# Differences of the values moved into the convolution stage, and queries and keys of two heads split together with their rows placed by DMA

## The chip, the cores and the metric

The kernel runs on one core of one Trainium2 chip. The metric is the time of one execution in microseconds of the device. Before the change three timed runs took 2573.38, 2568.3 and 2574.95 us, the median is 2573.38. One further execution was profiled.

## What is computed

The reference is one layer of a hybrid decoder trunk on x of 1024 tokens by 1024 channels, in float32. The change lies in its first sub-layer, parallel token mixing. One input projection of the normalised stream gives q, k and v of 16 attention heads of 64 dimensions, the inputs z, x, B, C and dt of a state-space mixer (SSD), and two gates, ga and gs. The x|B|C channels go through a causal convolution over 4 tokens and a silu. The attention is of the stick-breaking kind:

```
z = einsum('bhtd,bhsd->bhts', qf, kf)            # qf scaled by 64 ** -0.5
log_1mb = where(causal, log_sigmoid(-z), 0.0)
tail = cumsum(log_1mb, axis=3, reverse=True)
w = where(causal, exp(z + tail), 0.0)
out = einsum('bhts,bhsd->bhtd', w, v)
```

The outputs of attention and mixer are projected, gated and summed. Cross-attention into 256 memory tokens and a SwiGLU feed-forward follow.

The kernel computes the product of (1 - beta) from the right by a scan: with c[t, s] the product over j >= s of sigmoid(-z), the weight w[t, s] is c[t, s+1] - c[t, s]. So the sum over s of w[t, s] v[s] can be written with the differences v[s] - v[s+1], or rather of neighbouring rows of v, and c - 1. The "differences" below are these: rows r of v_d less rows r + 1, where v_d is v in DRAM with one row more.

## The kernel before the change

Every matmul is made in a reduced float32 format (F32R). An operand is split into a high half, its value rounded to F32R, and a low half, what is left of it, and a product takes three matmuls (high by high, low by high, high by low) or, where the two halves are stacked on the 128 rows that are contracted, two. The helpers are `hi_sb` (line 87), which writes a high half on POOL ("p"), DVE ("v") or ACT ("a"), and `lo_of` (line 98), which subtracts it from the value, on DVE or POOL.

The program is written with tile pools; the order of the instructions on each engine is set by a scheduler that follows the order of the code by its priorities, and a tile that is asked for from a full pool waits until the oldest one is released. All DMAs of the stages here are issued on SP's queue in order.

The work runs in stages, by the trace: norms, transposes and token-major projections (z, v) to 270 us; the convolution stage, 270 to 642 us; the attention, 624 to 1083 us, overlapping a little with its neighbours; SSD to 1480 us; output projections, cross-attention and feed-forward to the end at 2567 us.

**The convolution stage.** It makes 18 calls of `pair` (line 681). A pair computes 256 channels for all 1024 tokens with seven products in place of eight, each of 12 matmuls of 128x512 (`winograd_pair`, L226; matmuls L220 to L222), out of weights prepared by `winograd_weights` (L188): two loads of 512 KB (`wr`), four sums on POOL (`sf`, L196 to L199), then for each of seven operands a high half on ACT (L96) and a low half on DVE (L99) into `sw`. The products leave PSUM by three ACT copies (L230, L232, L234) and three DVE additions (L237, L239, L241) and one more ACT copy (L688) into two tiles of 128x1024, `y`, from the pool "b4" with six buffers. Twelve pairs are x|B|C channels, for which `conv` takes a further b4 buffer and makes three shifted multiply-adds on DVE (L667), the sigmoid on ACT (L668), and the product on DVE (L669); `tail` transposes the result in the next pair. Six pairs are gates: a sigmoid (L678) and a store to g_d (L679). The list `order` mixes them, one gate pair after every two of the others, with the last gate pair at the end.

**The attention.** It goes over 16 heads in eight pairs. A pair's q and k come from `qk_proj` (L782): `dense` (L758) makes 24 matmuls of 128x512 for each half of the tokens, so that a PSUM tile holds 64 rows of one head over 64 rows of the other. `ev_q` copies each head's rows to the upper half of its tile `qs` on ACT (L794) and writes the low half below it on DVE (L795). `ev_k` writes the high half into the upper rows of `kh` (L806) and the low half into those of `kl` (L807), and a DMA copies each to the lower 64 rows (L808, L809), so that two matmuls make a score: the stacked q with `kh` twice over, and with `kl` twice over.

A head is worked through in two m-steps, one per half of the tokens, so a pair has four. In each, `interleave` mixes three lists: `values` for this m-step, `scores` for the next one, and a quarter of the q and k projections of a later pair. `scores` has four blocks of two matmuls per 512 keys (L849, L850), a sigmoid on ACT (L851) and a scan on DVE over up to 1024 keys (L852, with the 0/1 tile `mask`). `values` transposes the result (L868), writes high and low halves `wth` on ACT (L871) and `wtl` on DVE (L872), and makes two matmuls with `v` (L880, L881), three steps behind the transposes; ACT and DVE bring the result out (L888, L889).

`differences` (L822) provides `v`. For each pair it loads two shifted tiles `va` and `vb` of 512 KB (L828), subtracts them on POOL (L829), and for each head writes the high half (L92) and the low half (L99) on POOL into a tile of two buffers.

## Time and profile before

| | |
|---|---|
| three timed runs | 2573.38, 2568.3, 2574.95 us |
| profiled execution | 2569.1 us, span 2567.4 us |
| mean granted clock of TensorE | 0.993 |
| busy: PE, DVE, ACT, POOL | 2485.3, 1817.7, 1149.7, 824.6 us |
| convolution window 280 to 640: PE, DVE, ACT, POOL | 356.33, 266.19, 193.84, 112.27 us |
| attention window 690 to 1000: PE, DVE, ACT, POOL | 299.81, 273.42, 195.80, 57.13 us |
| PE's wait for DVE in the attention window | 11.0 us |

A row of a group reads: line, engine, operation, output and inputs by the program's names, shape, count, then busy time and the mean of one in ns, then the idle time of the engine just before these instructions with what ended it. A row of the waits reads: who waited for whom, us in total, times, and the longest. A row of a timeline gives the start, the duration, and in brackets the idle time before with what ended it. "SPq" is the queue of SyncE, which issues the DMAs.

### The profile page before, as it was taken

Reading aid. Unit: us, or ns where it says so; the run is one execution under the profiler, and the core shown is the slowest. Engines: PE = TensorE matmul, PEld = TensorE weight load, DVE = VectorE, ACT = ScalarE, POOL = GpSimd, SP = SyncE. Lnnn points to the kernel's source line nnn. Section 1 sums busy time; section 2 is a strip of 40 time slices with the busy share of each in tenths; the row PEclk is TensorE's granted clock in tenths of the full one; section 3 lists DMA queues with packets and bytes.
Section 4 is the critical chain, followed back from the end, with each engine's and each line's share of the span. In section 5 each row is a group of like instructions: output and inputs, shape, how many; then the busy total and the mean of one; then the engine's idle time right before and its main releaser. Section 6 shows DMA issues by size and latency. Waiting matters only on the chain.

```text
span 2567.4 us, 32619 instructions
## 1 busy us (share of the span) xinstructions
PE 2485.3 (97%) x12026; PEld 2059.4 (80%) x12026; DVE 1817.7 (71%) x2143; ACT 1149.7 (45%) x2052; POOL 824.6 (32%) x666
## 2 busy tenths in 40 slices
PE   8999999999999999989999999999999999999998
PEld 6788788887788788777888788888787888887776
DVE  7685777767689898678788654415459666666997
ACT  6343455655466666556544302314233333334433
POOL 4331533221211121135655231100114333333675
PEclk9999999999999999989999999999999999999999
DMA  6441433333322222355332452321332232234322
GB/s 227 148 154 58 152 123 99 109 109 121 99 79 67 83 73 63 102 161 185 112 93 71 148 176 94 116 63 36 115 111 70 79 95 74 88 93 164 132 99 99
DMA packets 244331, 278.54 MB, mean 108 GB/s; under 512 B 15040, under 2 KB 171849, under 8 KB 243787
## 3 DMA queue, kind: packets, MB, share of 16 engines
q1 hardware_dynamic: 244170, 276.45, 34.0%
q8 instruction: 95, 1.56, 0.2%
q14 instruction: 66, 0.53, 0.1%
HBM read 197.87 MB, written 70.13 MB: 104 GB/s over the span
## 4 chain that ended last, share of the span: by engine, by line
PE 37%; DVE 7%; DMA 3%; issue 2%; POOL 1%; ACT 1%; SPq 0%; POOLq 0%; DVEq 0%; ACTq 0%
PE mm L222 5%; PE mm L220 5%; PE mm L221 5%; PE mm L102 4%; PE mm L104 3%; PE mm L103 3%; PE p L102 2%; PE p L103 2%; PE p L104 2%; DVE op L99 2%; PE pd L1090 1%; DMA gr<-gu_d 1%; DVE a L1755 1%; PE p L1468 1%; DMA wraw<-in_w_mix_out_dram 1%
## 5 line engine op out<-in xcount | busy, mean ns | idle before, releaser
L852 DVE TENSOR_TENSOR_SCAN n<-n,mask 128x128 f32<-128x128 f32 (+7 forms) x128 | 176.4, 1403 | 11.9 <-ACT n L851 9.2
L196 POOL TENSOR_TENSOR sf<-wr,wr 128x512 f32<-128x512 f32 x38 | 60.4, 1590 | 351.5 <-DMA wr<-in_w_gu_dram 129.3
L99 DVE TENSOR_TENSOR sw<-sf,sw 128x512 fp32r<-128x512 f32 x150 | 111.4, 754 | 58.9 <-ACT sw L96 58.4
L871 ACT ACTIVATE wth<-tr,mone 128x512 fp32r<-128x512 f32 x192 | 110.9, 580 | 73.3 <-PE tr L868 71.6
L96 ACT ACTIVATE sw<-sf 128x512 fp32r<-128x512 f32 x150 | 92.1, 626 | 106.8 <-PE mm L222 95.3
L872 DVE SCALAR_TENSOR_TENSOR wtl<-tr,wth 128x512 fp32r<-128x512 f32 x192 | 101.5, 546 | 40.0 <-ACT wth L871 38.5
L96 ACT ACTIVATE sw<-wr 128x512 fp32r<-128x512 f32 x113 | 70.8, 629 | 125.8 <-PE mm L222 124.2
L222 PE MATMUL mm<-h,sw 128*128 128x512 f32 x320 | 124.3, 389 | 1.8 <-DVE sw L99 1.8
L220 PE MATMUL mm<-h,sw 128*128 128x512 f32 x320 | 122.4, 391 | 3.1 <-ACT h L96 2.3
L221 PE MATMUL mm<-h,sw 128*128 128x512 f32 x320 | 124.5, 389 | 0.0
L102 PE MATMUL mm<-oth,bw 128*128 128x512 f32 (+1 forms) x320 | 122.0, 381 | 2.0 <-DVE a L1149 1.7
L104 PE MATMUL mm<-oth,bw 128*128 128x512 f32 (+1 forms) x320 | 119.1, 372 | 0.7 <-DVE bw L1136 0.5
L103 PE MATMUL mm<-otl,bw 128*128 128x512 f32 (+1 forms) x320 | 118.4, 370 | 0.0
L99 DVE TENSOR_TENSOR sw<-wr,sw 128x512 fp32r<-128x512 f32 x113 | 100.1, 889 | 16.1 <-ACT sw L96 16.1
L851 ACT ACTIVATE n<-sc 128x512 f32<-128x512 f32 (+1 forms) x192 | 89.1, 486 | 49.0 <-PE sc L850 25.0
L667 DVE SCALAR_TENSOR_TENSOR b<-b,prmT,b 128x1023 f32<-128x1023 f32 (+2 forms) x72 | 101.8, 1416 | 10.7 <-ACT b L665 10.2
L92 POOL TENSOR_SCALAR v<-va 128x512 fp32r<-128x512 f32 x16 | 20.0, 1255 | 273.7 <-PE av L881 147.9
L165 POOL TENSOR_SCALAR rstd<-ms 128x1 f32<-128x1 f32 x82 | 27.9, 341 | 244.6 <-ACT x L1370 103.5
L102 PE MATMUL p<-bw,h 128*128 128x512 f32 x256 | 98.9, 391 | 3.3 <-DVE x L1372 2.4
L104 PE MATMUL p<-bw,h 128*128 128x512 f32 x256 | 100.1, 392 | 0.0
L103 PE MATMUL p<-bw,h 128*128 128x512 f32 x256 | 99.8, 390 | 0.0
L198 POOL TENSOR_TENSOR sf<-wr 128x512 f32<-128x512 f32 x38 | 63.0, 1657 | 114.0 <-DVE sw L99 114.0
(592 smaller groups left out, 8141.5 us busy)
## 6 DMA issues: line engine op xcount, KB each, us to landing
wr<-in_w_gu_dram SPq DMA_DIRECT2D x80, 256.0 KB
wr<-in_w_in_dram SPq DMA_DIRECT2D x36, 512.0 KB
zr<-in_w_in_dram SPq DMA_DIRECT2D x32, 512.0 KB
gu_d<-t SPq DMA_DIRECT2D x44, 256.0 KB
wraw<-in_w_in_dram SPq DMA_DIRECT2D x20, 512.0 KB
xs_d<-b SPq DMA_DIRECT2D x32, 256.0 KB
s<-xs_d SPq DMA_DIRECT2D x32, 256.0 KB
s<-zs_d SPq DMA_DIRECT2D x32, 256.0 KB
```

Source lines behind the costliest of these rows:

```text
L96: A.activation(o, i, AF.Copy)
L99: eng.tensor_tensor(o, i, hi.bitcast(F32), ALU.subtract)
L102: first = T.matmul(ps, sh, mh, start=start, stop=False)
L103: T.matmul(ps, sh, ml, start=False, stop=False)
L104: T.matmul(ps, sl, mh, start=False, stop=stop)
L220: T.matmul(ps, w[0][:, k, :], b[0][:, k, :], start=first and k == 0, stop=False, skip_group_check=True)
L221: T.matmul(ps, w[0][:, k, :], b[1][:, k, :], start=False, stop=False, skip_group_check=True)
L222: T.matmul(ps, w[1][:, k, :], b[0][:, k, :], start=False, stop=last and k == 3, skip_group_check=True)
L667: V.scalar_tensor_tensor(acc[:, sh:], y[:, :S - sh], cw(3 - sh, f), acc[:, sh:], ALU.mult, ALU.add)
L852: V.tensor_tensor_scan(nt[:, 0:L][:, ::-1], nt[:, 0:L][:, ::-1], mask[:, S - L:][:, ::-1], 1.0, ALU.mult, ALU.max)
L871: A.activation(wh[:, t0 * P:], pt[:, t0 * P:], AF.Identity, bias=mone)
L872: V.scalar_tensor_tensor(wl[:, t0 * P:], pt[:, t0 * P:], -1.0, wh[:, t0 * P:].bitcast(F32), ALU.add, ALU.subtract)
```

## The change

It has two parts.

First, `differences` moves into the convolution stage. A new DRAM tensor `dv_d` holds for each head 64 columns of high halves and 64 of low halves for each token. After the products of a gate pair the code calls the new `differences(hp)`, twice after each of the first two gate pairs and once after each of the other four. It takes two buffers of the pool "b4", loads the two shifted tiles of v (L686 in the new numbering), subtracts on DVE (L690), and for each of two heads writes the high half on ACT and the low half on DVE (L100) and stores 512 KB to `dv_d` (L697). In the attention, `values_of` is one load of 512 KB for each head (L867). The subtraction and the splits on POOL are gone, and so are the tiles `va` and `vb`.

Second, for all pairs but the first, the 128 rows of a q or k result are split at once: one ACT copy to `hT` and one DVE subtraction to `lT` (L814), one buffer each. All rows of `qs`, `kh` and `kl` are then written by DMAs of 64x512 out of `hT` and `lT`: four for a half of q (L829) and eight for a half of k (L848), 24 for a pair where there were eight.

The core of the diff:

```diff
@@ -65,6 +65,7 @@
     bt_d = [scr(f"bt_d{g}", [S, P]) for g in range(NG)]
 
     v_d = scr("v_d", [S + 1, D])
+    dv_d = scr("dv_d", [S, NH * P])
     g_d = scr("g_d", [2 * D, S])
     o_d = scr("o_d", [D, S])
 
@@ -678,7 +679,26 @@
                 A.activation(y, y, AF.Sigmoid)
                 nc.sync.dma_start(g_d[f * P:(f + 1) * P, :], y)
 
-            def pair(c0, f, fin, npool):
+            def differences(hp):
+
+                va, vb = [mk(t4, [P, S], F32, "b4") for _ in range(2)]
+                for t, r in ((va, 0), (vb, 1)):
+                    nc.sync.dma_start(t.rearrange("p (c d) -> p c d", d=P),
+                                      v_d[r:S + r, hp * P:(hp + 1) * P].rearrange("(c p) d -> p c d", p=P))
+
+                def split():
+                    V.tensor_tensor(va, va, vb, ALU.subtract)
+                    dv = va.rearrange("p (c d) -> p c d", d=P)
+                    for j, t in enumerate((vb, va)):
+                        vt = t.bitcast(F32R).rearrange("p (c d) -> p c d", d=P)
+                        hi_sb(vt[:, :, 0:HD], dv[:, :, j * HD:(j + 1) * HD], "a")
+                        lo_of(vt[:, :, HD:P], dv[:, :, j * HD:(j + 1) * HD], vt[:, :, 0:HD])
+                        h = 2 * hp + j
+                        nc.sync.dma_start(dv_d[:, h * P:(h + 1) * P].rearrange("(c p) d -> p c d", p=P), vt.bitcast(F32))
+
+                return split
+
+            def pair(c0, f, fin, npool, beside=()):
                 ws = winograd_weights(rp, sfp, swp, adjacent(c0), npool)
                 y = [mk(t4, [P, S], F32, "b4") for _ in range(2)]
                 ys = [[t[:, 0:HALF], t[:, HALF:S]] for t in y]
@@ -688,6 +708,8 @@
                 A.activation(ys[1][0], p, AF.Copy)
                 fin(f, y[0])
                 fin(f + 1, y[1])
+                for h in beside:
+                    differences(h)()
 
             jobs = [(C_X + f * P, f, conv) for f in list(range(16, 24, 2)) + list(range(0, 16, 2))]
             gts = [(C_GA + f * P, f, gate) for f in range(0, 16 - LATE_GATES, 2)]
@@ -713,10 +735,13 @@
 
             for j in range(2):
                 nc.sync.dma_start(dts[:, j], dts_d[j])
+            todo = NH // 2
             for i, j in enumerate(order):
                 if i == 8:
                     dt_columns()
-                pair(*j, 3 if i == 0 else 0)
+                n = 0 if j[2] is not gate else 2 if todo > 5 else 1
+                pair(*j, 3 if i == 0 else 0, range(NH // 2 - todo, NH // 2 - todo + n))
+                todo -= n
             while pend:
                 tail(*pend.pop(0))
 
@@ -783,30 +808,49 @@
                 for j in range(2):
                     heads[2 * hp + j] = {}
 
+                def split(ps):
+                    hi, lo = [mk(t2, [P, HALF], F32R, n, bufs=1) for n in ("hT", "lT")]
+                    A.activation(hi, ps, AF.Copy)
+                    V.tensor_tensor(lo, ps, hi.bitcast(F32), ALU.subtract)
+                    return hi.bitcast(F32), lo.bitcast(F32)
+
                 def ev_q(ps, half):
                     sl = slice(half * HALF, (half + 1) * HALF)
+                    if hp > 0:
+                        parts = split(ps)
                     for j in range(2):
                         hd = heads[2 * hp + j]
                         if half == 0:
                             hd["q"] = mk(qk, [P, S], F32R, "qs")
-                        pj = ps[j * HD:(j + 1) * HD]
                         q = hd["q"]
-                        A.activation(q[0:HD, sl], pj, AF.Copy)
-                        V.tensor_tensor(q[HD:P, sl], pj, q[0:HD, sl].bitcast(F32), ALU.subtract)
+                        rows_ = slice(j * HD, (j + 1) * HD)
+                        if hp > 0:
+                            for r, t in enumerate(parts):
+                                nc.sync.dma_start(q[r * HD:(r + 1) * HD, sl].bitcast(F32), t[rows_])
+                        else:
+                            A.activation(q[0:HD, sl], ps[rows_], AF.Copy)
+                            V.tensor_tensor(q[HD:P, sl], ps[rows_], q[0:HD, sl].bitcast(F32), ALU.subtract)
 
                 def ev_k(ps, half):
                     sl = slice(half * HALF, (half + 1) * HALF)
+                    if hp > 0:
+                        parts = split(ps)
                     for j in range(2):
                         hd = heads[2 * hp + j]
                         if half == 0:
                             hd["kh"] = mk(qk, [P, S], F32R, "kh")
                             hd["kl"] = mk(qk, [P, S], F32R, "kl")
-                        pj = ps[j * HD:(j + 1) * HD]
                         kh, kl = hd["kh"], hd["kl"]
-                        A.activation(kh[0:HD, sl], pj, AF.Copy)
-                        V.tensor_tensor(kl[0:HD, sl], pj, kh[0:HD, sl].bitcast(F32), ALU.subtract)
-                        nc.sync.dma_start(kh[HD:P, sl].bitcast(F32), kh[0:HD, sl].bitcast(F32))
-                        nc.sync.dma_start(kl[HD:P, sl].bitcast(F32), kl[0:HD, sl].bitcast(F32))
+                        rows_ = slice(j * HD, (j + 1) * HD)
+                        if hp > 0:
+                            for d, t in zip((kh, kl), parts):
+                                for r in range(2):
+                                    nc.sync.dma_start(d[r * HD:(r + 1) * HD, sl].bitcast(F32), t[rows_])
+                        else:
+                            A.activation(kh[0:HD, sl], ps[rows_], AF.Copy)
+                            V.tensor_tensor(kl[0:HD, sl], ps[rows_], kh[0:HD, sl].bitcast(F32), ALU.subtract)
+                            for t in (kh, kl):
+                                nc.sync.dma_start(t[HD:P, sl].bitcast(F32), t[0:HD, sl].bitcast(F32))
 
                 return dense(C_Q + hp * P, ev_q), dense(C_K + hp * P, ev_k)
 
@@ -817,28 +861,16 @@
                     nc.sync.dma_start(g_d[gi * P:(gi + 1) * P, half * HALF:(half + 1) * HALF], gt)
                 return dense(C_GA + gi * P, ev)
 
-            dvs = {}
-
-            def differences(h):
-
-                j = h % 2
-                if j == 0:
-                    va, vb = [mk(vp, [P, NCH, P], F32, n, bufs=1) for n in ("va", "vb")]
-                    for t, r in ((va, 0), (vb, 1)):
-                        nc.sync.dma_start(t, v_d[r:S + r, h * HD:(h + 2) * HD].rearrange("(c p) d -> p c d", p=P))
-                    G.tensor_tensor(va, va, vb, ALU.subtract)
-                    dvs[0] = va
-                dv = dvs[0][:, :, j * HD:(j + 1) * HD]
-                vt = mk(vp, [P, NCH, P], F32R, "v")
-                hi_sb(vt[:, :, 0:HD], dv, "p")
-                lo_of(vt[:, :, HD:P], dv, vt[:, :, 0:HD], G)
-                heads[h]["v"] = vt
+            def values_of(h):
+
+                vt = heads[h]["v"] = mk(vp, [P, NCH, P], F32R, "v")
+                nc.sync.dma_start(vt.bitcast(F32), dv_d[:, h * P:(h + 1) * P].rearrange("(c p) d -> p c d", p=P))
 
             def scores(h, half, tb, ns_):
                 def run():
                     hd = heads[h]
                     if half == 0 and tb == 0:
-                        differences(h)
+                        values_of(h)
                     b = half * 4 + tb
                     L = (b + 1) * P
                     nt = mk(bp, [P, (half + 1) * HALF], F32, f"n{half}")
```

What this does to the rows of three queues. On DVE in the convolution stage, around the end of the first gate pair, stood before (`sw` are low halves of weights, `mm` a product in PSUM, the others b4 tiles):

```order
L669 TENSOR_TENSOR b_471_2717<-b_471_2717,b_466_2614 128x1024
L99 TENSOR_TENSOR sw_3047<-wr_3035,sw_3047 128x512
L241 TENSOR_TENSOR b_485_2758<-b_485_2758,mm_2761 128x512
L99 TENSOR_TENSOR sw_3048<-sf_3039,sw_3048 128x512
L239 TENSOR_TENSOR b_486_2759<-b_486_2759,mm_2760 128x512
L99 TENSOR_TENSOR sw_3049<-sf_3040,sw_3049 128x512
L99 TENSOR_TENSOR sw_3050<-wr_3036,sw_3050 128x512
L237 TENSOR_TENSOR b_511_2923<-b_511_2923,mm_2966 128x512
L99 TENSOR_TENSOR sw_3051<-sf_3041,sw_3051 128x512
```

and now:

```order
L690 TENSOR_TENSOR b_498_2891<-b_498_2891,b_499_2892 128x1024
L670 TENSOR_TENSOR b_471_2718<-b_471_2718,b_466_2615 128x1024
L100 TENSOR_TENSOR sw_3070<-wr_3058,sw_3070 128x512
L100 TENSOR_TENSOR b_499_2892<-b_498_2891,b_499_2892 128x8x64
L242 TENSOR_TENSOR b_485_2759<-b_485_2759,mm_2762 128x512
L100 TENSOR_TENSOR sw_3071<-sf_3062,sw_3071 128x512
L100 TENSOR_TENSOR b_498_2891<-b_498_2891 128x8x64
L100 TENSOR_TENSOR sw_3072<-sf_3063,sw_3072 128x512
L240 TENSOR_TENSOR b_486_2760<-b_486_2760,mm_2761 128x512
L100 TENSOR_TENSOR sw_3073<-wr_3059,sw_3073 128x512
L238 TENSOR_TENSOR b_515_2946<-b_515_2946,mm_2989 128x512
L100 TENSOR_TENSOR sw_3074<-sf_3064,sw_3074 128x512
```

A subtraction of 128x1024 (L690) stands ahead of the product of the convolution, the two low halves of the differences stand between the low halves of the weights, and the subtraction of the next difference is the row behind these.

On DVE in the attention, at the first half of a key of one head pair, stood before (`n` is a score tile, so L852 is the scan; `wtl` the low half of the transposed weights):

```order
L807 TENSOR_TENSOR kl_7577<-mm_7452,kh_7576 64x512
L852 SCALAR_TENSOR_TENSOR n_1420_7607<-n_1420_7607,mask_5486 128x640
L872 SCALAR_TENSOR_TENSOR wtl_7513<-tr_7507,wth_7512 128x512
L872 SCALAR_TENSOR_TENSOR wtl_7532<-tr_7527,wth_7531 128x384
L807 TENSOR_TENSOR kl_7583<-mm_7452,kh_7582 64x512
L852 SCALAR_TENSOR_TENSOR n_1426_7628<-n_1426_7628,mask_5486 128x768
L852 SCALAR_TENSOR_TENSOR n_1432_7648<-n_1432_7648,mask_5486 128x896
```

and now:

```order
L814 TENSOR_TENSOR lT_7694<-mm_7570,hT_7693 128x512
L884 SCALAR_TENSOR_TENSOR n_1458_7728<-n_1458_7728,mask_5575 128x640
L904 SCALAR_TENSOR_TENSOR wtl_7630<-tr_7624,wth_7629 128x512
L904 SCALAR_TENSOR_TENSOR wtl_7649<-tr_7644,wth_7648 128x384
L884 SCALAR_TENSOR_TENSOR n_1464_7749<-n_1464_7749,mask_5575 128x768
L884 SCALAR_TENSOR_TENSOR n_1470_7769<-n_1470_7769,mask_5575 128x896
L904 SCALAR_TENSOR_TENSOR wtl_7661<-tr_7657,wth_7660 128x256
```

The two subtractions of 64 rows have become one of 128 rows, at the place of the first; the scans and the low halves keep their order.

On SP, for the two halves of the keys of the same head pair, stood before:

```order
L808 DMA kh_7576<-kh_7576 64x512
L809 DMA kl_7577<-kl_7577 64x512
L808 DMA kh_7582<-kh_7582 64x512
L809 DMA kl_7583<-kl_7583 64x512
L808 DMA kh_7576<-kh_7576 64x512
L809 DMA kl_7577<-kl_7577 64x512
L808 DMA kh_7582<-kh_7582 64x512
L109 DMA wraw_8260<-in_w_in_dram 128x8x128
L809 DMA kl_7583<-kl_7583 64x512
```

and now:

```order
L848 DMA kh_7697<-hT_7693 64x512 x2
L848 DMA kl_7698<-lT_7694 64x512 x2
L848 DMA kh_7703<-hT_7693 64x512 x2
L848 DMA kl_7704<-lT_7694 64x512 x2
L867 DMA v_7850<-dv_d 128x8x128
L848 DMA kh_7697<-hT_7823 64x512 x2
L848 DMA kl_7698<-lT_7824 64x512 x2
L848 DMA kh_7703<-hT_7823 64x512 x2
L848 DMA kl_7704<-lT_7824 64x512 x2
```

Each half has eight transfers instead of four, out of `hT` and `lT` (a row marked x2 is two), and the load of one head's differences stands between the two halves.

## Prediction

> **What bounds the kernel now.** I read first the page's busy shares, then the table of windows for the two stages that the change touches, then PE's waits in them, then the timelines around those waits, and last the groups of DVE, ACT and POOL that the change removes or adds.
>
> ```profile
> PE 2485.3 (97%) x12026; PEld 2059.4 (80%) x12026; DVE 1817.7 (71%) x2143; ACT 1149.7 (45%) x2052; POOL 824.6 (32%) x666
> ...
> 280.00:640.00 360.00, 356.33 (x1652) 295.59 (x1651) 266.19 (x279) 193.84 (x294) 112.27 (x69) 1.00 0.37 116
> 690.00:1000.00 310.00, 299.81 (x1639) 250.69 (x1640) 273.42 (x335) 195.80 (x381) 57.13 (x36) 1.00 0.26 72
> ```
>
> The first line says that PE is busy 97% of the span. The two windows (columns: us, then busy time of PE, PEld, DVE, ACT, POOL, then granted clock, DMA share, GB/s) are the convolution stage and six head pairs of the attention. PE leaves 3.7 us of 360 idle in the one and 10.2 us of 310 in the other. DVE is at 74% and 88%, POOL at 31% and 18%. A change that gives PE no other work can therefore win at most PE's idle time, and PE's waits say what that consists of. The first three lines are the attention's, the next four the convolution's (the fourth is a group of ACT, with its idle time at the end), the last two those from 1000 to 1130 us:
>
> ```profile
> PE av L881 <- DVE wtl L872: 8.6, 12, 1.2
> PE mm L102 <- DVE qs L795: 1.4, 1, 1.4
> PE tr L868 <- DVE wtl L872: 1.0, 1, 1.0
> ...
> PE mm L220 <- ACT b L230: 2.7, 1, 2.7
> DVE sw L99 <- ACT sw L96: 31.1, 18, 4.5
> DVE b L239 <- PE mm L222: 20.0, 9, 3.6
> L232 ACT ACTIVATE b<-mm 128x512 f32<-128x512 f32 x18 | 10.8, 601 | 2.1 <-DMA g_d<-b 2.1
> ...
> PE dec L1038 <- DMA colrows<-sum_d: 6.4, 1, 6.4
> PE av L881 <- DVE wtl L872: 1.9, 3, 1.2
> ```
>
> In the attention PE waits only for DVE, 11.0 us in all: 12 times for the low half of the transposed weights, twice in each of the six pairs. In the convolution it hardly waits at all; there DVE and ACT wait for PE. What DVE does ahead of the long one of the two waits (first fence DVE, second PE):
>
> ```profile
> 743.71 0.68 DVE L807 TENSOR_TENSOR kl<-mm,kh 64x512 fp32r<-64x512 f32 x1
> 744.36 1.49 DVE L852 TENSOR_TENSOR_SCAN n<-n,mask 128x640 f32<-128x640 f32 x1
> 745.77 1.13 DVE L872 SCALAR_TENSOR_TENSOR wtl<-tr,wth 128x512 fp32r<-128x512 f32 x2
> 746.92 0.69 DVE L807 TENSOR_TENSOR kl<-mm,kh 64x512 fp32r<-64x512 f32 x1
> 747.54 3.66 DVE L852 TENSOR_TENSOR_SCAN n<-n,mask 128x768 f32<-128x768 f32 x2
> 751.23 0.62 DVE L872 SCALAR_TENSOR_TENSOR wtl<-tr,wth 128x256 fp32r<-128x256 f32 x2
> ```
>
> ```profile
> 750.23 0.28 PE L850 MATMUL sc<-kl,qs 128*128 128x256 f32 x1
> 751.71 0.38 PE L881 MATMUL av<-wtl,v 128*128 128x256 f32 x1 [1.20 <-DVE wtl L872]
> ...
> 777.04 0.39 PE L881 MATMUL av<-wtl,v 128*128 128x256 f32 x1 [0.22 <-DVE wtl L872]
> ```
>
> DVE works without a gap from 743.71 to 751.85: two low halves of a key, one 640 scan, two wtl, two long scans (grouped in one row), and then the wtl for which PE stands 1.20 us. One m-step later the same happens with two query halves, and PE stands 0.22 us. Six pairs of 1.20 and 0.22 make 8.5 of the 8.6 us.
>
> **The change part by part.** *One split for two heads.* A projection's PSUM result is 128 rows, and was split in two 64-row pieces, each an ACT copy and a DVE subtraction. Now one copy and one subtraction take all 128 rows:
>
> ```profile
> L807 DVE TENSOR_TENSOR kl<-mm,kh 64x512 fp32r<-64x512 f32 x26 | 17.9, 688 | 2.3 <-ACT kh L806 0.5
> L795 DVE TENSOR_TENSOR qs<-mm,qs 64x512 fp32r<-64x512 f32 x24 | 16.5, 689 | 1.5 <-ACT qs L794 0.5
> L872 DVE SCALAR_TENSOR_TENSOR wtl<-tr,wth 128x512 fp32r<-128x512 f32 x77 | 52.2, 679 | 23.9 <-ACT wth L871 23.4
> ```
>
> A 128-row subtraction out of PSUM costs what a 64-row one does (679 against 688 ns), so half of the 34.4 us of L795 and L807 goes: 17.2 us of DVE in the window. Of this only what stands in the gapless run ahead of a PE wait counts. The second kl of the run (0.69) disappears and no other is put there, so the wtl at 751.23 comes 0.69 earlier and the wait falls from 1.20 to 0.51. The first kl stays, since it needs the end of the same matmul as before. The wait of 0.22 behind two qs is covered by one of them and goes. Per pair that is 0.69 + 0.22 = 0.91 us, over six pairs 5.5 us. The single wait of 1.4 for a qs, which is the second of two pieces, should fall by one piece, 0.7; the last pair's wait (1.2 of the 1.9 us) by 0.69 once more. Sum: 5.5 + 0.7 + 0.7 = 6.9 us. What is late next is the same wtl, by the scans. Bounds: nothing, if the wait is only refilled, and 11.0 + 1.9 = 12.9 us, if all of the waits for DVE go.
>
> *Values off POOL.* Ahead of this stands what POOL did for them:
>
> ```profile
> L829 POOL TENSOR_TENSOR va<-va,vb 128x1024 f32<-128x1024 f32 x6 | 19.0, 3175 | 28.7 <-DMA va<-v_d 23.8 <-issue 4.9
> L92 POOL TENSOR_SCALAR v<-va 128x512 fp32r<-128x512 f32 x12 | 16.2, 1350 | 236.2 <-PE av L881 124.5 <-PE tr L868 111.7
> L99 POOL TENSOR_TENSOR v<-va,v 128x512 fp32r<-128x512 f32 x12 | 15.5, 1292 | 1.0
> L852 DVE TENSOR_TENSOR_SCAN n<-n,mask 128x640 f32<-128x640 f32 x13 | 19.4, 1492 | 0.2
> ```
>
> It loses 50.7 us of its 57 here, but PE waits for no v, and POOL waits 236 us for PE. So the removal is worth nothing directly. It could be worth something if POOL slowed DVE; the 13 scans of 640 average 1492 ns, and the one above took 1.49 us while POOL did nothing, so I see no slowing and take 0. The Trainium skill ("SBUF — State Buffer", Who interferes with whom) states that a DVE instruction with two SBUF inputs contends with a GpSimd instruction that reads SBUF, and that the one that comes second is blocked. The scan has two such inputs, so by this rule there would be a gain that my sum leaves out; it is a rival below. The row of the 640 scans does not bear it out.
>
> *Differences in the convolution.* Eight times a 128x1024 subtraction and two 128x512 low halves on DVE, two high halves on ACT, and on SP's queue two loads and two stores of 512 KB. The nearest rows of that stage:
>
> ```profile
> L99 DVE TENSOR_TENSOR sw<-sf,sw 128x512 fp32r<-128x512 f32 x69 | 53.1, 774 | 16.2 <-ACT sw L96 15.9
> L99 DVE TENSOR_TENSOR sw<-wr,sw 128x512 fp32r<-128x512 f32 x52 | 50.1, 970 | 15.2 <-ACT sw L96 15.2
> L669 DVE TENSOR_TENSOR b<-b,b 128x1024 f32<-128x1024 f32 x24 | 34.1, 1420 | 13.1 <-ACT b L668 13.1
> L96 ACT ACTIVATE sw<-sf 128x512 fp32r<-128x512 f32 x68 | 42.7, 629 | 35.9 <-PE mm L222 30.9 <-POOL sf L197 2.4 <-POOL sf L196 1.3
> ```
>
> DVE: 8 x (1.42 + 2 x 0.87) = 25 us, with 0.87 as the middle of 774 and 970; ACT: 16 x 0.63 = 10 us. DVE goes from 266 to 291 of 360 us, ACT from 194 to 204. PE's own order there has nothing new. The work is hidden by the 94 us that DVE stands idle, more than half of it behind PE or ACT's splits (20.0 and 31.1 us). What may not be hidden is the new wait: the subtraction waits for two loads, and behind it in DVE's order stand the low halves of the next weights and the sums out of PSUM, for which PE's next products wait. How long a load takes, and how long SP needs for each of its issues:
>
> ```profile
> 731.65 0.37 SPq L828 DMA_DIRECT2D va<-v_d  x1
> 736.42 3.34 POOL L829 TENSOR_TENSOR va<-va,vb 128x1024 f32<-128x1024 f32 x1 [4.80 <-DMA va<-v_d]
> ...
> 743.71 0.47 SPq L808 DMA_DIRECT2D kh<-kh  x1
> 744.43 0.47 SPq L809 DMA_DIRECT2D kl<-kl  x1
> ```
>
> The load of 512 KB landed 4.8 us after its issue. The differences also take two of the six b4 buffers, so that a later pair's PSUM sums may have to wait for a store, as one did for g_d (2.1 us on ACT, hidden from PE). Bounds for PE: -2.7 us, if the one wait there (L230) goes with the new order of buffers, and 8 x 2.7 = 21.6 us, if each difference brings such a wait. I take 0.3 us for each, 2.4 in all, near the low end, because in 18 pairs with six buffers in rotation a late evacuation cost PE something only once.
>
> *Rows placed by DMA.* For a pair there are now 24 transfers of 128 KB on SP's queue instead of 8, and two loads of v instead of va and vb. At 0.72 us from issue to issue (743.71 to 744.43) the eight of a key half take 5.8 us. Their landing is seen only where PE waited for one, at a crowded place:
>
> ```profile
> 664.66 0.55 SPq L808 DMA_DIRECT2D kh<-kh  x1
> ...
> 669.72 0.30 PE L849 MATMUL sc<-kh,qs 128*128 128x128 f32 x1 [0.39 <-DMA kh<-kh]
> ...
> 706.86 0.59 ACT L806 ACTIVATE kh<-mm 64x512 fp32r<-64x512 f32 x1 [1.62 <-PE mm L104]
> 718.62 0.59 ACT L794 ACTIVATE qs<-mm 64x512 fp32r<-64x512 f32 x1 [0.25 <-PE mm L104]
> ```
>
> There it took up to 5.1 us. The next split of the shared hT and lT buffers, which the transfers must have read by then, comes 11.8 us later (706.86 to 718.62). Of those some 1.3 (0.59 on ACT, 0.69 on DVE) go by until hT and lT are written: 11.8 - 1.3 = 10.5 against 5.8 + 5.1 = 10.9. A transfer as slow as that would miss it by 0.4 us, one that lands in 4.7 would not. The steady part has a DMA share of 0.26, so I take 0. Bounds: 0 and 7 x 0.4 = 2.8 us. The Trainium skill ("DMA: Bandwidth & Descriptors", Rules for kernel authors) says that two transfers to disjoint partition halves serialize, and that one of 128 partitions should be used instead. This speaks against the 16 further halves of each pair, and by it the sum would lie at the 2.8 us end; no row of this trace shows two halves in flight with nothing else beside them, so it is not borne out here nor refuted.
>
> *The joins.* The new buffers shift the addresses of the attention and of the stage behind it, and the last gate pair's stores now stand ahead of the first loads of the attention. Each can move the waits there (2.7 us of L220, 0.39 at 669.72, 6.4 of L1038) either way; I take 0, with 3 us on both sides.
>
> Sum: -6.9 + 2.4 = -4.5 us. The profiled execution took 2569.1 us with a span of 2567.4, 4.3 us under the median of the three timed runs, 2573.38, which lie 6.6 us apart. Their mean with the profiled one is 2571.4; 4.5 less is 2567, and the median less 4.5 is 2569, so I say 2568.
>
> **Rivals.** About 0.3%, 7.7 us, is what a measurement of this kernel can tell from no change.
>
> *All waits for DVE go (0.36).* DVE falls from 88% to about 83% of the attention (17.2 of 310 us). If that slack adds up over the m-steps, all 12.9 us vanish, and the 2.7 of L220 with them; less 2.4, that is 13.2 us: 2559. A second way to the same end is that POOL did slow DVE: the 50.7 us that leave POOL lay beside 16% of the window, so beside some 44 of DVE's 273 us, and if those get shorter the waits go too, but PE cannot gain more than its waits, 2559 again. That would be the skill's rule on the shared port, named above. Against both: with the kl gone the two long scans still stand ahead of the wtl, and the 640 scans show no slowing.
>
> *The convolution pays (0.14).* The in-order subtraction holds DVE while its loads are under way. If each of the eight costs PE what the one late evacuation did, 2.7 us, the sum is -6.9 + 21.6 = +14.7: 2587, counted like all of these from 2572.5, which is the forecast without its gain. It turns slower from (6.9 + 7.7) / 8 = 1.8 us per difference. For it: 4.8 us of landing, and only six buffers. Against it: DVE waits for PE there.
>
> *Placement comes late (0.06).* If transfers land 2 us later than at the crowded place, ACT waits 2.4 us at hT with the sigmoids and the high halves of the weights behind it, in 7 pairs: 16.8 - 4.5 = +12: 2585.
>
> *It does nothing (0.06).* PE is at 97% and the waits are refilled by the scans: 2573.
>
> **How the numbers follow.** The forecast, -4.5 us, has 0.38. With the 3 us of the joins on both sides it lies between -7.5 and -1.5, all within 0.3%, and its own range is 2565 to 2571. With the case of nothing that makes 0.44 for the same; 0.36 are for faster, 0.14 + 0.06 = 0.20 for slower. The range of 8 in 10 reaches down over most of the case in which all waits go, to 2556, and up into the convolution's case, to 2582.
>
> **What would show it.** In the attention the long wait at av falls from 1.20 to about 0.5 and the short one is gone, while the scans keep 1492 ns; POOL is nearly empty there. In the convolution DVE is near 81%, and PE's waits stay under 6 us. It is wrong if PE waits in the convolution behind ACT's or DVE's evacuations more than a few times, if the av wait is as long as before, if ACT waits at hT for a DMA, or if the 640 scans become shorter.

## The result and the profile after

The changed kernel takes 2569.5 us (median of 22 runs, 2564.66 to 2573.03), the kernel before 2572.55 us (22 runs, 2567.41 to 2577.59). The ratio is 0.9986 with a 95% interval of 0.9979 to 0.9992, that is 2 to 5 us faster. The forecast was 2568 us, 4.5 us faster.

The profiled execution of the changed kernel has a span of 2569.0 us. It is longer than that of the profile before (2567.4) though the kernel is faster in the timed runs, so single executions have to be read by stage. First the busy line of the page, then the windows of the two stages:

```profile
PE 2487.9 (97%) x12026; PEld 2063.5 (80%) x12026; DVE 1810.5 (70%) x2139; ACT 1139.1 (44%) x2040; POOL 759.9 (30%) x626
...
280.00:640.00 360.00, 355.54 (x1631) 293.39 (x1630) 283.45 (x299) 201.00 (x305) 111.28 (x69) 1.00 0.51 155
690.00:1000.00 310.00, 301.56 (x1647) 253.41 (x1647) 250.12 (x311) 176.78 (x356) 6.28 (x6) 1.00 0.45 116
```

In the attention DVE fell from 273.42 to 250.12 us and POOL from 57.13 to 6.28, and PE gained 1.75 us of busy time. In the convolution DVE rose by 17 and ACT by 7 us. PE's waits, first in the convolution window, then in the attention's:

```profile
PE mm L221 <- ACT b L231: 3.0, 2, 2.4
PE tr L658 <- DVE b L670: 0.8, 2, 0.4
PE mm L221 <- ACT b L708: 0.7, 1, 0.7
...
PE av L913 <- DVE wtl L904: 4.6, 6, 0.8
PE av L912 <- DVE oT L921: 3.2, 6, 0.5
PE tr L900 <- DVE wtl L904: 0.7, 1, 0.7
```

In the convolution 4.5 us stand where 3.7 stood. In the attention the short wait for the wtl is gone and the long one, once a pair, is 0.8 instead of 1.2 us. But there is a wait that did not exist before: six times 0.5 us for oT, the tile into which DVE brings a finished result out of the PSUM bank `av`. What DVE does around both, in one pair, and PE at the ends of the two waits:

```profile
739.00 0.69 DVE L904 SCALAR_TENSOR_TENSOR wtl<-tr,wth 128x512 fp32r<-128x512 f32 x1 [1.09 <-ACT wth L903]
740.37 0.68 DVE L921 TENSOR_TENSOR oT<-av,gt 64x512 f32<-64x512 f32 x1 [0.67 <-ACT gt L920]
...
745.02 0.69 DVE L814 TENSOR_TENSOR lT<-mm,hT 128x512 fp32r<-128x512 f32 x1 [0.37 <-ACT hT L813]
745.68 1.49 DVE L884 TENSOR_TENSOR_SCAN n<-n,mask 128x640 f32<-128x640 f32 x1
747.09 1.13 DVE L904 SCALAR_TENSOR_TENSOR wtl<-tr,wth 128x512 fp32r<-128x512 f32 x2
748.13 3.66 DVE L884 TENSOR_TENSOR_SCAN n<-n,mask 128x768 f32<-128x768 f32 x2
751.72 0.59 DVE L904 SCALAR_TENSOR_TENSOR wtl<-tr,wth 128x256 fp32r<-128x256 f32 x2
```

```profile
739.48 0.22 PE L913 MATMUL av<-wtl,v 128*128 128x128 f32 x1
739.53 1.04 PE L900 MATMUL tr<-ident,n 128*128 128x128 f32 x8
741.10 0.50 PE L912 MATMUL av<-wth,v 128*128 128x512 f32 x1 [0.53 <-DVE oT L921]
...
751.05 0.33 PE L912 MATMUL av<-wth,v 128*128 128x256 f32 x1
752.16 0.38 PE L913 MATMUL av<-wtl,v 128*128 128x256 f32 x1 [0.78 <-DVE wtl L904]
```

The run of DVE from the split of a key to the wtl is one subtraction shorter: the wtl starts 6.70 us after the split (745.02 to 751.72), before the change 7.52 us (743.71 to 751.23). The wait for it fell by only 0.4 us, because PE runs out of work earlier too, 6.36 us after the split instead of 6.80: a value matmul that ran behind the projection's last matmuls now runs ahead of them (742.89 in the profile before, 743.27 now), and two score matmuls that stood ahead of the wait now stand behind it (750.11 and 750.23 before, 753.60 and 753.72 now).

The wait for oT comes from another shift on PE: three projection matmuls that stood between the transposes before the change (738.83 in the profile before) now run ahead of the last value matmul of the m-step. Eight transposes are then all that PE has (739.53) until the only PSUM bank of `av` is emptied, and it stands 0.53 us for oT.

### The profile page after: what moved, and what is told of

It is laid out like the page before. It is cut to its first block, busy times and chain, and to the rows that moved or that the text cites. A ratio compares the mean times of both kernels' runs of the same rounds, so it can differ in the third digit from the quotient of the medians.

```text
span 2569.0 us, 32803 instructions
## 1 busy us (share of the span) xinstructions
PE 2487.9 (97%) x12026; PEld 2063.5 (80%) x12026; DVE 1810.5 (70%) x2139; ACT 1139.1 (44%) x2040; POOL 759.9 (30%) x626
## 5 line engine op out<-in xcount | busy, mean ns | idle before, releaser
L884 DVE TENSOR_TENSOR_SCAN n<-n,mask 128x128 f32<-128x128 f32 (+7 forms) x128 | 169.7, 1346 | 19.7 <-ACT n L883 19.6
L100 DVE TENSOR_TENSOR sw<-sf,sw 128x512 fp32r<-128x512 f32 x150 | 113.9, 770 | 57.8 <-ACT sw L97 57.4
L93 POOL TENSOR_SCALAR whi<-wraw 128x1024 fp32r<-128x1024 f32 x10 | 10.9, 1087 | 413.2 <-DVE wtl L904 242.6
L100 DVE TENSOR_TENSOR sw<-wr,sw 128x512 fp32r<-128x512 f32 x113 | 97.8, 868 | 20.5 <-ACT sw L97 20.4
L100 DVE TENSOR_TENSOR zl<-zr,zh 128x512 fp32r<-128x512 f32 x84 | 73.0, 880 | 34.9 <-ACT zh L97 34.8
```

Source lines behind the costliest of these rows:

```text
L100: eng.tensor_tensor(o, i, hi.bitcast(F32), ALU.subtract)
L884: V.tensor_tensor_scan(nt[:, 0:L][:, ::-1], nt[:, 0:L][:, ::-1], mask[:, S - L:][:, ::-1], 1.0, ALU.mult, ALU.max)
```

## The experiments

The profiles are compared by a common clock: PE has 12026 matmul records in each kernel, in nearly the same order, so the starts of the 1000th, 2500th, 5200th and 7000th record cut the program into a stretch of the convolution (333.3 us in the first profile before), one from there to the end of the attention (532.0), the SSD (344.5) and the rest (what lies before the first cut and behind the last). The second stretch begins about 100 us before the convolution stage ends. Differences below are against that profile. The attention also has a clock of its own, the distance between the first score matmuls of successive pairs.

### The same two kernels again

Both were run once more without an edit, the kernel before first.

> The kernel before once more, unchanged, for a second profile of it. My theory: the times of its convolution and attention stages come out within 0.5 us of the first profile, since their waits are set by the order of the program, and the 3 to 6 us by which its executions differ lie behind the attention. Rival: the attention itself varies by 2 us or more, so that gains of that size cannot be read from single profiles.

> The changed kernel once more, unchanged. My theory: again 2 us more than before in the convolution and some 3 us less from the end of the convolution to the end of the attention; its 4.5 us of loss in the SSD stage do not repeat. Rival: the loss in the SSD stage repeats, so it belongs to the change, by the new order and addresses there.

Timed, against the same runs of the kernel before: 0.9991 (0.9980 to 1.0002) for the kernel before itself, 0.9981 (0.9971 to 0.9990) for the changed one. The stretches:

| | convolution | to the end of the attention | SSD | rest |
|---|---|---|---|---|
| before, again | -0.5 | +3.2 | +0.4 | -2.1 |
| changed, first | +1.8 | -3.3 | +4.5 | -1.3 |
| changed, again | +1.0 | -3.4 | +2.3 | -1.9 |

For the kernel before, the rival is right: its attention differs by 3.2 us between two executions. For the changed kernel my theory is: -3.3 and -3.4. The pairs are 49.65 us apart in the kernel before, except that one pair in the first profile takes 51.3 and three in the second take 51.0 to 51.5. In the changed kernel every steady pair takes 49.4 to 49.6. Its loss in the SSD came back by half, so there neither theory holds as a whole. What makes the long pairs is seen in the second profile before, PE's waits first, then two moments of POOL and DVE, the disturbed one last, and PE behind it:

```profile
PE av L881 <- DVE wtl L872: 8.6, 12, 1.2
PE mm L102 <- DVE qs L795: 3.8, 3, 1.4
PE tr L868 <- DVE wtl L872: 1.1, 1, 1.1
```

```profile
787.34 3.35 POOL L829 TENSOR_TENSOR va<-va,vb 128x1024 f32<-128x1024 f32 x1 [4.80 <-DMA va<-v_d]
787.27 1.21 DVE L852 TENSOR_TENSOR_SCAN n<-n,mask 128x512 f32<-128x512 f32 x1
...
887.90 2.39 POOL L829 TENSOR_TENSOR va<-va,vb 128x1024 f32<-128x1024 f32 x1 [4.67 <-DMA va<-v_d]
887.97 3.40 DVE L852 TENSOR_TENSOR_SCAN n<-n,mask 128x512 f32<-128x512 f32 x1
891.40 0.69 DVE L795 TENSOR_TENSOR qs<-mm,qs 64x512 fp32r<-64x512 f32 x1
892.14 0.50 PE L102 MATMUL mm<-t1h,whi 128*128 128x512 f32 x1 [1.44 <-DVE qs L795]
```

At 787 the scan starts 0.07 us ahead of POOL's subtraction; it takes its 1.21 us, and the subtraction takes 3.35. At 887 the subtraction starts 0.07 us ahead; it takes 2.39 us, and the scan takes 3.40, ending 1.08 us after POOL. PE stands 1.44 us for the qs behind that scan. Whichever comes second waits for the whole of the other, and which one it is hangs on the landing of a load (the release in brackets). The three waits for qs in this profile, and the one of 1.4 us in the first, all follow such a scan: of the twelve 512 scans of the window one takes over 3 us in the first profile and three take 2.95 to 3.40 in the second, each beside L829. The Trainium skill ("SBUF — State Buffer", Who interferes with whom) states that a DVE instruction with two SBUF inputs contends with a GpSimd instruction that reads SBUF, and that whichever comes first blocks the other; the rows at 787 and 887 agree with both.

### No work for the values

```
vt = heads[h]["v"] = mk(vp, [P, NCH, P], F32R, "v")
c0 = h // 2 * P
nc.sync.dma_start(vt.bitcast(F32), v_d[0:S, c0:c0 + P].rearrange("(c p) d -> p c d", p=P))
```

> The kernel before, with the work for the values left out: each head's tile v is loaded from v in DRAM by one transfer, without subtraction and without split (so the attention's output is not the reference's). POOL loses its 40 instructions in the attention, nothing is added in the convolution, queries and keys are split as before. My theory (POOL's work cost nothing): PE waits for the wtl as before, 12 times and 8 to 9 us between 690 and 1000, and the time stays within 2 us of the kernel before. Rival (POOL slowed DVE's scans through a shared port): those waits fall by half or more, and the time by 4 us or more.

> The run without any work for the values once more (output not the reference's). My theory: from the end of the convolution to the end of the attention again 2 us less than in the kernel before; the stages behind are slower than in its first profile, since that execution was 5 us under its median. Rival: the stages behind are as in the first profile and the attention is where it varies.

Timed 1.0005 (0.9994 to 1.0015), and again 0.9993 (0.9982 to 1.0003). PE's waits in the window, second profile:

```profile
PE av L870 <- DVE wtl L861: 8.6, 12, 1.2
PE sc L839 <- DVE kl L807: 0.6, 1, 0.6
PE sc L839 <- DMA kl<-kl: 0.3, 1, 0.3
```

The waits for the wtl are as before to the tenth, as I expected, so nothing that POOL does reaches the wtl. But no wait for a qs is left, no 512 scan is long (they average 1214 ns, before 1390 and 1714), and all steady pairs but the last take 49.6 to 50.1 us in the two profiles. To the end of the attention it is 2.1 and 1.3 us under the first profile before, and 5.3 and 4.5 us under the second. The rival had the right mechanism and the wrong place. The timed runs show no gain; in both profiles the SSD, where the instructions stand in another order, takes it back with +3.0 and +3.4 us.

There is a second place in which POOL slowed DVE. The scans of 128 columns, in the kernel before and in the first profile of this one:

```profile
L852 DVE TENSOR_TENSOR_SCAN n<-n,mask 128x128 f32<-128x128 f32 x12 | 9.2, 768 | 0.0
L841 DVE TENSOR_TENSOR_SCAN n<-n,mask 128x128 f32<-128x128 f32 x12 | 4.8, 400 | 0.0
```

All twelve are slowed, to between 765 and 770 ns, each by the last 0.50 us of a high half on POOL (L92). No wait of PE hangs on them, since the waits for the wtl are the same without them.

### The split of queries and keys alone

The kernel of the last experiment, with the changed kernel's `ev_q` and `ev_k`.

> Queries and keys split at once and placed by DMA as in the changed kernel, with the values' work left out everywhere as in e_none (output not the reference's); nothing is added in the convolution. My theory: against the kernel before, 5 to 7 us faster, ratio 0.9973 to 0.9981, all of it between the start and the end of the attention; the convolution takes what it took before; the changed kernel's 3 us are this gain less 2 to 3 us of cost in the convolution. Rival (the gain in the attention is POOL's relief): no faster than e_none.

> Queries and keys split at once, without any work for the values, once more (output not the reference's). My theory: the attention again 0 to 1 us shorter than without the split, so that most of the 8 us between these two kernels' timed runs lie behind the attention. Rival: the attention's gain is 4 us or more in this profile, and the first one was not typical.

Timed 0.9974 (0.9965 to 0.9983), and again 0.9969 (0.9958 to 0.9980): 7 to 8 us faster than the kernel before, as expected, and so not the rival. Yet the profiles do not put this where I did. Steady pairs take 49.53 us, against 49.65 without the split, so the split is worth 0.1 us per pair. To the end of the attention it is -2.3 and -3.7 us, on average 1.3 under the same kernel without the split, and in the second profile by itself 2.0, more than its theory and less than its rival. PE's waits of the window, against 8.6 for the wtl without the split:

```profile
PE av L914 <- DVE wtl L905: 4.7, 6, 0.8
PE av L913 <- DVE oT L922: 3.2, 6, 0.5
PE tr L901 <- DVE wtl L905: 0.7, 1, 0.7
```

4 us less of the one, 3.2 of the other. More than that lies in the SSD, where this kernel does not have the loss of 3 us of the kernel without the split (-0.5 and +1.0 against +3.0 and +3.4).

### The differences alone

> The first part of the change alone: differences in the convolution stage and one load of them for each head, queries and keys split for each head as before. My theory: 1.5 to 3 us lost in the convolution by late evacuations behind the stores of the differences, nothing won in the attention, the 12 waits for wtl stay: ratio 1.0000 to 1.0015. Rival (the values' move is where the gain comes from): 3 us faster or more, ratio 0.9988 or less.

The edit puts the old `ev_q` and `ev_k` into the changed kernel. Timed 1.0008 (0.9999 to 1.0018). The convolution lost 1.7 us, the waits for the wtl are 8.6 us in 12, as expected. PE does stand where a store has to land: in the first profile of the changed kernel ACT waited for one, and PE 0.54 us behind it.

```profile
325.59 0.60 ACT L231 ACTIVATE b<-mm 128x512 f32<-128x512 f32 x1 [5.58 <-DMA dv_d<-b]
```

```profile
326.24 0.50 PE L221 MATMUL mm<-t2h,sw 128*128 128x512 f32 x1 [0.54 <-ACT b L231]
```

In the second profile of the changed kernel this wait is missing, and its convolution loses 1.0 us instead of 1.8.

What I had not expected is the attention: -2.1 us, the same as without any work for the values, and steady pairs of 49.62 to 49.71 us with none disturbed; no 512 scan of the window takes over 1.22 us. The move of the differences does win something there, by taking POOL's subtraction away from the scans. In this profile the SSD (+1.8) and the rest (+4.5 us) lose more than that, and in the timed runs the first part alone wins nothing.

### One difference at a time

```
n = 1 if j[2] is gate or i in (9, 12) else 0
```

> The changed kernel with one difference after each of the six gate pairs and one after each of two convolution pairs (the 10th and the 13th), so that none has two. My theory (the cost in the convolution comes from the second of two differences, whose store a later pair's y has to wait for): the 0.9 and 1.1 us that PE lost near 325 and 367 are gone and nothing comes in their place; the stage takes 1.5 to 2 us less than in the changed kernel, ratio 0.9976 to 0.9981. Rival (any use of two b4 buffers costs this): PE loses about as much at other pairs, ratio as for the changed kernel, 0.9982 to 0.9990, or worse, since a convolution pair needs four b4 buffers itself.

Timed 0.9985 (0.9976 to 0.9995), as the changed kernel. The convolution lost 1.8 us as well. PE's losses near 325 and 367 are gone (ACT still waits for stores of dv_d, 5.1 us in three places, but PE not behind it). In their place a wait for a tail near 424 us, which PE had before the change with 1.0 us, has become 2.3:

```profile
PE tr L658 <- DVE b L670: 2.5, 2, 2.3
PE mm L221 <- ACT b L231: 2.4, 1, 2.4
```

So the rival holds in this trial: the stage loses about as much at another place. Whether it is the buffers or the 21 us of further work on DVE that move the loss there was not taken apart.

### The subtraction made twice

```
for _ in range(2):
    V.tensor_tensor(lo, ps, hi.bitcast(F32), ALU.subtract)
```

> The changed kernel with the one subtraction that writes lT made twice (the second writes the same again), so that DVE has as many instructions for queries and keys as before the change; ACT, the DMAs and the convolution stay as changed. My theory (the gain is the DVE instruction that left the run ahead of the wtl): the long wait at the value matmuls grows back from 0.8 to 1.2 us or more in each pair, and with the new waits for oT the time is 3 to 6 us over the changed kernel's: ratio to the kernel before 1.0000 to 1.0012. Rival (the gain comes from the shorter ACT work or the earlier release of PSUM): within 1 us of the changed kernel, ratio 0.9982 to 0.9990.

Timed 1.0048 (1.0036 to 1.0060), more than either theory said. 28 more subtractions of 0.69 us, 19 us of DVE, made the stretch to the end of the attention 11.8 us longer than in the changed kernel, and pairs are 51.0 to 51.6 us apart:

```profile
PE av L914 <- DVE wtl L905: 6.1, 11, 0.7
PE av L913 <- DVE oT L922: 3.2, 6, 0.5
PE sc L883 <- DMA kl<-lT: 1.9, 4, 1.1
```

The wait grew as the theory says in sign, but to 6.1 us in 11 places of up to 0.7, not to 1.2 in six; with lT later its transfers are late as well. A DVE instruction put into this stage costs PE 0.4 us, and one taken out did not give that back. The run is not the exact mirror of the change, though: the second subtraction stands right behind the first and ahead of lT's transfers, while the one that the change took out of a key's split stood a scan and two wtl later.

### Other orders for PE

The changed kernel with `(s1, 0, 0.6)` for the scores, and with `PIN = 10`:

> The changed kernel with the scores of the next m-step spread over the first 0.6 of an m-step instead of 0.7; in PE's order, three projection matmuls or a pair of score matmuls then stand between the last value matmul of one m-step and the first of the next, where the changed kernel has only transposes. My theory (the six new waits of 0.5 us for oT come from that order on PE alone): these waits are gone, 3 us, and the wait of 0.8 us for the wtl shrinks or stays: 2 to 5 us faster than the changed kernel, ratio to the kernel before 0.9965 to 0.9978. Rival (the new waits come from DVE or ACT being late with the evacuation of av): they stay at 6 times 0.5 us, and the time is the changed kernel's.

> The changed kernel with projection matmuls held behind the tenth last score or value matmul in place of the eighth last, which brings three projection matmuls between the transposes ahead of the first value matmul of an m-step. My theory (the waits for oT are PE's order alone): the six waits of 0.5 us are gone; if the waits for wtl stay at 4.6 us in the window, the time is 2 to 4 us under the changed kernel's, ratio 0.9970 to 0.9978. Rival (the order of PE only moves waits between oT and wtl, as the run with scores over 0.6 did): the waits for wtl grow by as much, ratio 0.9984 or more.

Timed 1.0030 (1.0017 to 1.0042) and 1.0118 (1.0105 to 1.0131). PE's waits of the first, then of the second:

```profile
PE av L913 <- DVE wtl L904: 11.3, 15, 1.1
PE tr L900 <- DVE wtl L904: 0.7, 1, 0.7
PE sc L881 <- DMA kh<-hT: 0.4, 1, 0.4
```

```profile
PE sc L881 <- DMA kh<-hT: 9.6, 6, 2.0
PE sc L881 <- ACT n L883: 5.3, 11, 0.7
PE av L912 <- DVE oT L921: 3.9, 11, 0.4
PE av L913 <- DVE wtl L904: 2.8, 5, 0.6
```

In the first the waits for oT are gone, so they do come from PE's order; the waits for the wtl grew from 4.6 to 11.3 us, so the sum is worse, and pairs take 50.6 us. In the second the waits for oT went on, which my theory did not foresee, and the projections come so late that the scores wait for the transfers of kh, up to 2.0 us each. This is near the third rival of the prediction, placement that comes late, but not the same: there ACT was to wait at hT, and in no run does it wait there for a transfer.

### Differences in the attention, in halves

```
va, vb = [mk(vp, [P, NCH, HD], F32, n, bufs=1) for n in ("va", "vb")]
...
G.tensor_tensor(va, va, vb, ALU.subtract)
...
```

> Queries and keys as in the changed kernel, but the differences stay in the attention on POOL, for each head by itself, in tiles of half the size (which the SBUF has room for beside hT and lT); nothing is added in the convolution. My theory (part two is all of the gain, part one only a cost): as e_split, 5 to 7 us faster than the kernel before, ratio 0.9973 to 0.9981, and faster than the changed kernel. Rival (POOL's work beside DVE or its eight more loads on SP's queue cost as much as the convolution's differences do): as the changed kernel, 0.9984 to 0.9990.

Timed 1.0004 (0.9994 to 1.0014): worse than my theory and than the rival, which had the right direction. The split is there, the convolution is untouched (-0.5 us), but POOL's subtraction is again beside the scans, now of 128x512 and twice as often, and each of the twelve in the window slows one scan. Of the twelve 512 scans four take 1.73 to 1.99 us; one of them and its neighbour on POOL:

```profile
934.59 1.74 DVE L889 TENSOR_TENSOR_SCAN n<-n,mask 128x512 f32<-128x512 f32 x1
```

```profile
933.23 2.02 POOL L869 TENSOR_TENSOR va<-va,vb 128x512 f32<-128x512 f32 x1 [3.03 <-issue]
```

The other eight subtractions run beside scans of 384 columns, which then take 1.98 to 2.05 us; one that runs alone takes 0.93:

```profile
L889 DVE TENSOR_TENSOR_SCAN n<-n,mask 128x384 f32<-128x384 f32 x12 | 19.9, 1662 | 0.0
```

Pairs take 49.9 to 50.5 us, 0.3 to 0.9 more than with the split and no such work, and PE waits 6.3 us for the wtl in 14 places, against 4.7 in six. To the end of the attention the profile is still 1.7 us under the first one before; the rest of the timed loss lies behind it (SSD +1.2, rest +4.6 us in this profile), and its cause is open. Of the kernels that compute everything, the changed one and the one with one difference at a time are the fastest, and they are not told apart.

## Why the prediction was right, and where its terms were not

**The total.** -4.5 us was forecast, -3 (-2 to -5) was measured, and -5 the second time, with the same sign and within 0.3%. That the total came out is in part luck. In the attention, where the gain was to be, the two terms that make it were mis-sized in opposite directions, and a part of what the timed runs give to the split lies in a stage that it was not meant to touch.

**The terms by the timed runs.** The split is worth 6 to 8 us: 0.9974 and 0.9969 against 1.0005 and 0.9993 without work for the values, 0.9986 and 0.9981 against 1.0008 with the differences in the convolution. Taking the values' work away wins nothing by itself (1.0005 and 0.9993), and the differences in the convolution cost about 3 us (0.9986 and 0.9981 against 0.9974 and 0.9969). With intervals of some 2.5 us on each side of every ratio these agree with the forecast terms, -6.9, 0 and +2.4. The profiles say that the way was another, as follows.

**One split for two heads: -6.9 us forecast, about -1 found in the attention.** The mechanism is there: 17 us of DVE are gone, the run ahead of the wtl is 0.8 us shorter, the short wait vanished. Four things were wrong in the term. The long wait fell to 0.8 and not to 0.5 us, since PE came earlier as well. The sum had no place for a new wait: "no other is put there" was true of DVE, but the order of PE moved with it, and 6 x 0.5 us for oT took 3.2 of the 4.0 us back. The 0.7 us for the single wait for a qs were not the split's to win: behind that wait stood a 512 scan of 3.32 us, blocked by POOL. And the 0.7 us of the last pair were a misreading. It has no later keys to split; ahead of its wtl stands the low half of a weight (L99), which the change leaves as it was, and PE's waits for the wtl between 1000 and 1130 us are 1.9 us, as before:

```profile
1024.98 1.23 DVE L99 TENSOR_TENSOR wlo<-wraw,whi 128x1024 fp32r<-128x1024 f32 x1 [0.28 <-ACT whi L96]
...
PE av L913 <- DVE wtl L904: 1.9, 3, 1.2
```

The first line is of the kernel before, the second of the changed one.

In the profiles without work for the values the split wins 1.3 us to the end of the attention and 3 us in the SSD. The latter is most of what those profiles show, and no term of the sum stood for it.

**Values off POOL: 0 forecast, 3 to 4 us found in the attention's profiles, none in the timed runs.** On average of two profiles each, to the end of the attention the kernel without the values' work is 3.3 us under the kernel before (-2.1 and -1.3 against 0 and +3.2), and the differences alone, of which there is one profile, 3.7 (-2.1). The step that failed is the one in which the 640 scans stood for all scans. In neither profile before does one of them run beside any work for the values, so their mean of 1492 ns said nothing, and that it stayed at 1491 after the change said nothing either. L829 meets a 512 scan in all six pairs of the window, because there its loads land; the row that would have shown it is the group of those scans, mean 1390 ns where one alone takes 1210. The scans of 128 columns would have shown the slowing too: 768 ns in the profile before, more than the 682 of those of 256 columns. So in the attention the rule that I weighed and set aside moved more than the term I built the sum on. The rival that it stood in was right in its condition, that DVE beside POOL gets shorter, but its 2559 us did not come: only the waits for qs went, not those for the wtl. Its bound, the waits of the one profile, was too low for an execution with three collisions in place of one.

**Differences in the convolution: +2.4 us forecast, 1.3 to 2.3 us found.** The stretch is +1.8 and +1.0 in the changed kernel, +1.7 with the differences alone, and -0.3 to -0.5 in the kernels without them. The place was as described: an evacuation behind a store of dv_d. The price on DVE was read too high. The subtraction takes 1222 ns and not 1420, since the row of L669 mixes sixteen instructions of 1.21 to 1.23 us with eight that ran beside POOL's sums and took 1.47 to 2.31, the same slowing once more; and the low halves take 0.70 us and not 0.87. The eight differences cost DVE 21 us in place of 25. It was forecast at 81% of the window and is at 79%, with seven of the eight in it.

```profile
L690 DVE TENSOR_TENSOR b<-b,b 128x1024 f32<-128x1024 f32 x7 | 8.6, 1222 | 6.6 <-DMA b<-v_d 6.6
```

**Rows placed by DMA: 0 forecast, 0 found.** ACT waits at hT only for PE, and no score waits for a transfer in the window. The thin margin that the prediction worked out, at hT, was not reached in any run. A margin that it did not work out was: in the kernels that make the split twice or hold the projections back, scores wait for the transfers out of hT and lT, 1.9 and 9.6 us in the window, and 0.4 us with the scores spread over 0.6.

**The joins: 0 with 3 us on both sides.** The SSD is +4.5 and +2.3 us in the changed kernel's two profiles, 0 and +0.4 before. The first is more than the range I gave, and with the stretches up to there it would leave nothing of the gain in that profiled execution, while the timed runs have it. The order of PE in the SSD goes with its time: three profiles in which PE's records from the 5100th to the 7000th stand in the order of the kernel before (its own two and the subtraction made twice) have 0, +0.4 and +0.9; three in the order of the split alone (its own two and the differences in halves) -0.5, +1.0 and +1.2; the two without work for the values +3.0 and +3.4. Two profiles of one kernel differ by up to 2.2 us, though, and the kernel with one difference at a time, which has nearly the order of the kernel before, shows none of the loss (-1.1) and is no faster than the changed one in timed runs. No run took the SSD alone, so what the order costs there is not shown. Also open is a part of the 7 to 8 us by which the split without the values' work is faster in timed runs: its two profiles are on average 4 us under the two of the kernel before, which were executions 3.5 and 0.8 us under the medians of their runs.

## What to carry to other kernels

When a group of like instructions has one mean that is above that of its neighbours, look for the single long one and for what ran beside it on POOL, and look for a small shape that takes longer than a larger one, as 128 columns did here beside 256; a wait that appears once in a profile may appear three times in the next. A saving on an engine that is waited for is worth what is left after the scheduler has re-sorted the waiting engine: list the order of that engine too before summing. And where a stage has a repeating period, compare periods; here 49.65, 49.55 and 51.4 us told in one look what totals with 10 us of scatter could not. A period tells only of its stage, though: most of what the timed runs gave to the split did not show in it.

## What the runs showed of the hardware

A POOL subtraction of 128x1024 with both inputs in SBUF takes 2.39 us when it starts first and 3.35 us when a 512 scan on DVE started 0.07 us before it; the scan takes 1.21 us when first and 3.40 us when second. The second instruction waited for the whole of the first, and 0.07 us decided. The subtraction of half the size, 128x512, which takes 1.29 us when it starts first, still lengthened a scan of 512 columns to between 1.73 and 1.99 us and one of 384 from 0.93 to 2.05. A POOL instruction with a single SBUF input does it too: beside the high halves of v (L92), the scan of 128 columns took 0.77 us in all 24 cases of the two profiles before, and 0.40 us in the two without work for the values. A DVE subtraction of 128x512 out of PSUM takes 0.69 us, as one of 64x512 does.
